# The experts' loop of a DeltaNet-Conformer-MoE layer: gate and up product of a block in one piece, down product last, and no row added for empty slots

## The chip, the core and the metric

The kernel runs on one core of a Trainium2 chip. The core has a matrix engine (TensorE, PE in the profile, with its weight loads shown as PEld), a vector engine (VectorE, DVE), a scalar engine (ScalarE, ACT), a general engine (GpSimd, POOL) and a queue for transfers (SyncE, SP). Each engine works through its own list of instructions in order and waits on semaphores for the others. The metric is the device time of one execution in microseconds (us). The kernel before takes 1718.21 us, the median of three runs from 1717.66 to 1718.78.

## What is computed

One layer on 1024 latent tokens of width 1024, with 256 context tokens: a mixer (gated DeltaNet heads beside a convolution branch), then a mixture of experts, then a final norm. The change lies in the mixture of experts. Each token picks 6 of 64 experts; an expert is a small gated network from 1024 to 256 and back. Cut to that:

```python
def expert_block(args):
    tok, e = args
    return swiglu(h_pad[tok], w_gate[e], w_up[e], w_down[e])   # (silu(h wg) * (h wu)) wd

out = lax.map(expert_block, (slot_tok.reshape(n_blocks, MOE_BLOCK), block_exp))
weighted = (out.reshape(n_slots, d) * slot_w[:, None]).astype(h.dtype)
routed = jnp.zeros((t + 1, d), h.dtype).at[slot_tok].add(weighted)[:t]
return (routed + swiglu(hf, s_gate, s_up, s_down)).reshape(bsz, n, d)
```

There are 1024 x 6 = 6144 pairs of a token and an expert. All data is float32.

## The kernel before

The first part of the kernel (the mixer, the router, the shared expert) is recorded into a planner, which puts the operations of each engine into an order by the durations and dependencies that are written beside them. The experts' loop, which the change is about, stands behind the planner's output and is written out by hand.

**Blocks.** The experts are ranked by how many tokens chose them, and the list `CAPS` gives each rank a fixed number of places. `plan` packs these places into 62 blocks of 128 slots. A block is either 128 slots of one expert, or is shared by two: 96 and 32 slots, or 64 and 64. `split_units` then cuts a shared block into units of 32 or of 64 slots; a unit becomes a matrix product that uses 32 or 64 columns of the array, at a column position of its own (`tile_position`). Of the 62 blocks, 35 are whole (128 columns), 17 run in units of 32 and 10 in units of 64. Mostly a shared block and a whole one take turns. The places add up to 7936 slots, and 6144 of them hold a row; the others are empty.

**The steps of one block**, with the tiles that name them in the profile:

- `b_onehot` (line 1807, DVE) and `b_slots` (`sl`, lines 1815 to 1818, PE and DVE) find which token stands in each slot.
- `b_index` (lines 1827 to 1846) works out, on DVE, the rows to gather (`ig`) and the rows to add to (`ic`), with a small product on PE for the second expert of a shared block, and has POOL issue the gather of the token rows into `xg` (four buffers).
- `b_xpose` (`xt`, lines 1856 to 1862) transposes the gathered rows on PE; DVE and ACT move them into `hg` (two buffers) with the modulation applied.
- `b_weights` (line 1868, DVE) picks the routing weight of each slot.
- `b_gate_up` (`gu`, line 1608, PE) multiplies by the gate and up weights, in eight steps over the input width that sum into one bank. It can be called for a part of the eight steps.
- `b_swish` (`sg`, lines 1612 and 1613, ACT and DVE) makes silu(gate) x up.
- `b_actT` (`at`, lines 1618 and 1619) transposes that on PE; ACT copies it into `aT`.
- `b_down` (`dn`, line 1628, PE) multiplies by the down weights; DVE scales the result into `ob` (line 1887, two buffers).
- `b_add` (line 1896, POOL) issues an indirect transfer that adds the rows of `ob` to an accumulator in device memory. There are two accumulators, `acc_d[0]` and `acc_d[1]`; while blocks are shared the adds take turns between them, and in the last blocks all go to `acc_d[0]`. An add waits for the landing of the one before it on the same accumulator.

A float32 product of 128 rows and 512 columns stands in the trace as two matrix instructions. So `gu` of a whole block is 16 instructions, `dn` is 8, and in units of 32 there are four times as many, which run side by side on different columns.

**Empty slots.** In an empty slot the arithmetic of `b_index` gives the row number 1024 + slot for both lists. The gather has a bounds check at 1023 and leaves such rows out. The add has none: the accumulators have 1152 rows, and empty slots add their (unused) row to the last 128. `constants` (lines 1601 to 1603) sets these 128 rows to zero beforehand, by a memset of `ob[0]` and two copies.

**Weights.** Six slots hold the weights of six experts (3 MB each). SP fetches the next expert when a slot is free; the loop appends a slot to `free` when the last block of its expert has been issued.

**The order in the loop.** Iteration `i` works on several blocks at once: swish, `at`, `dn` and add of block `i`, `gu` of block `i + 1`, `xt` of `i + 2`, `sl` and index of `i + 4`, one-hot of `i + 5`. Since every engine takes its instructions in the order in which they are written, the order of the calls in the loop is the order on PE:

```python
at(b_swish, i)
at(b_gate_up, i + 1, 0, 2)
at(b_actT, i)
at(b_gate_up, i + 1, 2, 4)
at(b_down, i)
at(b_add, i, 0, None)
...
at(b_slots, i + 4)
at(b_xpose, i + 2, 0)
at(b_xpose, i + 2, 1)
at(b_weights, i + 2)
at(b_gate_up, i + 1, 4, 6)
at(b_index, i + 4)
at(b_gate_up, i + 1, 6, 8)
at(b_onehot, i + 5)
```

The loop starts with `i = -1`, which runs only the parts for later blocks. Behind it the accumulators are read back and summed, and the final norm is computed and stored.

Of the kernel before, what the change touches and what calls it, by code (L numbers as in the profile page):

```python
# [8 lines left out]
F32 = mybir.dt.float32  # L9
# [4 lines left out]
OP = mybir.AluOpType  # L14
# [135 lines left out]
def hybrid_kernel(tc, a, out):  # L150
    nc = tc.nc
    V, S, G, PE, SY = nc.vector, nc.scalar, nc.gpsimd, nc.tensor, nc.sync
    top = ExitStack()

    w = {n: a[n][0] for n in a if n not in ('x', 'c', 'ctx', 'c_ctx', 'g_final')}
# [5 lines left out]
    dp = top.enter_context(tc.tile_pool(name="dram", bufs=1, space=DR))  # L161
# [357 lines left out]
    O = Order()  # L519
    N = SimpleNamespace()  # L520

    def adder(eng, lat):
        def add(dur, fn, r=(), w=(), low=0):
            O(eng, dur, fn, r, w, low, lat)
        return add

    DVE, ACT, POOL, TE, DMA = (adder(*u) for u in (("DVE", 0.2), ("ACT", 0.2), ("POOL", 0.2), ("PE", 0.2), ("DMA", 2.2)))
# [534 lines left out]
    O = Order()  # L1062
# [134 lines left out]

    st_r, st_o = ExitStack(), ExitStack()
    xn_d = dp.tile([1024, 1088], F32, name="xn_d")
    acc_d = [dp.tile([1152, 1024], F32, name=f"acc{i}") for i in range(2)]  # L1200
    rs2 = cp.tile([128, 8, 2], F32, name="rs2")
    osc = cp.tile([128, 8, 4], F32, name="osc")

# [388 lines left out]
    def constants():  # L1592
        G.iota(N.iof, pattern=[[1, 128]], base=0, channel_multiplier=0, allow_small_or_imprecise_dtypes=True)
        G.iota(N.ioc, pattern=[[0, 128]], base=0, channel_multiplier=1, allow_small_or_imprecise_dtypes=True)
        for t in range(8):
            G.memset(N.aux[:, t, 0:1], float(128 * t - 1024))
        G.memset(N.aux[:, :, 2:3], 1.0)
        G.tensor_copy(N.aux[:, :, 1:2], N.ioc[:, 0:1][:, None, :].to_broadcast([128, 8, 1]))
        G.tensor_scalar(N.s1024[:, 0:1], N.ioc[:, 0:1], 1024.0, None, op0=OP.add)
        G.tensor_scalar(N.s1024[:, 1:2], N.ioc[:, 0:1], -1.0, None, op0=OP.mult)  # L1600
        G.memset(N.ob[0], 0.0)
        for i in range(2):
            SY.dma_start(acc_d[i][1024:1152], N.ob[0])

    def gate_up(pgu, lhsT, units, wts, ks=range(8)):
        for k in ks:
# [116 lines left out]
    for k in range(5, 10):  # L1723
# [9 lines left out]
        w=["wsg1"])  # L1733
    DMA(3.0, lambda: SY.dma_start(slots[3][0][:, 1], uw.rearrange("(p k) f -> p k f", k=8)), r=["wsg1"],
        w=["wsg"])
    DMA(3.0, lambda: SY.dma_start(slots[3][1], dw.rearrange("(p k) f -> p k f", k=2)), r=["wsg1"], w=["wsd"])
    DMA(1.5, lambda: SY.dma_start(N.gt2b, gt_d[8:16].rearrange("k p -> (k p)").partition_broadcast(128)), r=["open2"],
        w=["gt2"])
    O("POOL", 3.0, constants, r=["open2"], w=["ap", "so00", "so01"], lat=3.0)
    for k in range(2):  # L1740
        POOL(2.5, lambda k=k: G.tensor_tensor(slots[3][1][:, k, :], slots[3][1][:, k, :], N.gt2b, op=OP.mult),
             r=["gt2"], w=["wsd"], low=1)
# [45 lines left out]
    def fetch_ready():  # L1788
        while nxt and free:
            fetch(nxt.pop(0))  # L1790
# [101 lines left out]
    def b_add(B, j0, j1):  # L1892

        for (o, n, r, ic) in B['dst'][j0:j1]:
            turn[0] = 1 - turn[0] if B['two'] else 0
            G.indirect_dma_start(out=acc_d[turn[0]], out_offset=bass.IndirectOffsetOnAxis(ap=ic[:n], axis=0),  # L1896
                                 in_=B['ob'][o:o + n], in_offset=None, compute_op=OP.add)

    def o_overflow():

# [52 lines left out]
    def at(f, i, *a_):  # L1953
        if 0 <= i < nblk:
            f(BL[i], *a_)
# [42 lines left out]
    for i in range(-1, nblk):  # L1998
        fetch_ready()
        if 0 <= i + 1 < nblk:  # L2000
            BL[i + 1]['wts'] = {r: slots[held[r]] for (_, _, r) in BL[i + 1]['u3']}
        at(b_swish, i)
        at(b_gate_up, i + 1, 0, 2)
        at(b_actT, i)
        at(b_gate_up, i + 1, 2, 4)
        at(b_down, i)
        at(b_add, i, 0, None)
        if i >= 0:
            for r in {r for (_, _, r) in BL[i]['u3']}:
                if last[r] == i:  # L2010
                    free.append(held.pop(r))
            fetch_ready()
        if i < 0:
            at(b_slots, 2)
            at(b_index, 2)
        at(b_slots, i + 4)
        at(b_xpose, i + 2, 0)
        at(b_xpose, i + 2, 1)
        at(b_weights, i + 2)
        at(b_gate_up, i + 1, 4, 6)  # L2020
        at(b_index, i + 4)
        at(b_gate_up, i + 1, 6, 8)
        at(b_onehot, i + 5)
    ms_.close()


# [8 lines left out]
    with tc.For_i(0, n_over) as it:  # L2035
        rr = V.value_load(N.rows[0:1, bass.ds(it, 1)], min_val=0, max_val=63)
        re = SY.value_load(N.rows[0:1, bass.ds(it + 128, 1)], min_val=0, max_val=63)
        load_expert(0, re)
        V.tensor_tensor(pcol, N.posr[:, :, bass.ds(rr, 1)],
                        N.basb[:, bass.ds(it, 1)][:, None, :].to_broadcast([128, 8, 1]), op=OP.subtract)  # L2040
        oh = N.oh[0]
        V.tensor_tensor(oh, N.iol[:, None, 0:128].to_broadcast([128, 8, 128]), pcol.to_broadcast([128, 8, 128]),
                        op=OP.is_equal)
        B = dict(i=0, two=False, oh=oh, segs=[(0, 128, 0)], u3=[(0, 128, 0)], wts={0: slots[0]})
        b_slots(B)
        b_index(B)
        V.tensor_copy(wsel, B['xg'][:, bass.ds(rr + 1024, 1)])
        B['wc'] = wsel
        b_xpose(B, 0)
        b_xpose(B, 1)  # L2050
        b_gate_up(B, 0, 8)
        b_swish(B)
        b_actT(B)
        b_down(B)
        b_add(B, 0, None)
# [54 lines left out]
```

## Time and profile before

| | |
|---|---|
| median of three runs | 1718.21 us (1717.66 to 1718.78) |
| the profiled execution | 1718.04 us |
| its span | 1716.1 us |
| mean granted clock of TensorE in it | 0.975 |
| experts' gate, up and down weights fetched | 64 transfers of 1024 KB each |
| gathers of token rows, adds of result rows | 62 and 89 indirect transfers |

The span is the time from the first to the last instruction of the profiled execution; the runs' times have some 2 us more around it. A row of the timeline is one or several instructions of the same kind in a row: start in us from the span's start, length, engine, line, operation, the tiles written and read, active rows and columns of the array for a weight load or product, shape, and a count. The length of a merged row of PE reaches to the modelled end of its last instruction, which is later than the start of the next row; so the time that a piece costs is best read from start to start. In brackets stands the idle time of the engine just before, and what ended it.

### The profile page before, as it was taken

To read this page: it belongs to the slowest core of one execution; us is meant where nothing else is said; L and a number is where in the kernel's file an instruction comes from. 1 tells how busy PE (TensorE), PEld (TensorE's weight loads), DVE (VectorE), ACT (ScalarE), POOL (GpSimd) and SP (SyncE) were. 2 spreads that over 40 slices of the span, in tenths; PEclk is the share of its full clock that TensorE was granted. 3 is DMA by queue.
4 is the path that set the end of the run, shared out by engine and by line. 5 is a ranking of instruction groups with operands and counts; after the bars stand their busy time and mean duration, and the time that the engine had idled before them with its cause. 6 is when DMAs were issued, how large, how long until landed. Compare 5 with 4: busy or idle time off the path is not lost. (4 is left out here: it accounts for less than half of the span.)

```text
span 1716.1 us, 23373 instructions
## 1 busy us (share of the span) xinstructions
PE 1599.0 (93%) x8380; PEld 931.8 (54%) x8380; DVE 974.5 (57%) x2156; ACT 498.4 (29%) x1096; POOL 526.2 (31%) x443
## 2 busy tenths in 40 slices
PE   5999999896898899799999999999999999999995
PEld 1556766574775899787544334344444344343442
DVE  2576997498884976887603444343434444343424
ACT  4541267832222123444212112111111111111212
POOL 2321232442242776631111323232222223232310
PEclk9999999898999999899999999999999999999998
DMA  9455112554445136666458999999999999999957
GB/s 321 156 184 173 44 59 72 160 154 145 144 132 187 50 111 209 217 208 218 164 202 305 326 335 336 319 364 307 332 374 364 327 333 318 327 385 347 355 126 259
DMA packets 150657, 405.39 MB, mean 236 GB/s; under 512 B 21359, under 2 KB 64780, under 8 KB 125580
## 3 DMA queue, kind: packets, MB, share of 16 engines
q1 hardware_dynamic: 130978, 340.39, 54.6%
q0 software_dynamic: 18288, 59.26, 14.5%
q10 hardware_dynamic: 1274, 4.23, 0.6%
q8 instruction: 67, 1.10, 0.3%
q14 instruction: 50, 0.41, 0.1%
HBM read 340.01 MB, written 71.95 MB: 240 GB/s over the span
## 5 line engine op out<-in xcount | busy, mean ns | idle before, releaser
L1608 PE MATMUL gu<-wg,hg 128*32 128x512 f32 (+2 forms) x1968 | 463.2, 599 | 1.6 <-ACT hg L1862 1.6
L1887 DVE SCALAR_TENSOR_TENSOR ob<-dn,wc,gt2b 128x512 f32<-128x512 f32 x124 | 93.1, 751 | 366.0 <-PE dn L1628 366.0
L1896 POOL DMA_INDIRECT acc<-ob,ic x89 | 134.5, 1512 | 527.5 <-DVE st L1818 466.9
L1608 PEld LDWEIGHTS gu<-wg,hg 128*32 128x32 f32 (+2 forms) x1968 | 148.7, 137 | 203.9 <-issue 159.0
L1628 PE MATMUL dn<-wd,sg 128*32 128x512 f32 (+2 forms) x984 | 226.8, 598 | 0.5 <-ACT sg L1619 0.5
L1862 ACT ACTIVATE hg<-xt,mf 128x128 f32<-128x128 f32 x248 | 93.2, 456 | 377.3 <-PE xt L1856 376.0
L1628 PEld LDWEIGHTS dn<-wd,sg 128*32 128x32 f32 (+2 forms) x984 | 78.0, 137 | 143.3 <-issue 142.6
L676 PE MATMUL bk<-hTh,whi 128*128 128x512 f32 (+1 forms) x320 | 125.0, 391 | 12.2 <-ACT ot L762 9.4
L676 PE MATMUL bk<-hTl,whi 128*128 128x512 f32 (+1 forms) x320 | 120.0, 375 | 0.0
L676 PE MATMUL bk<-hTh,wlo 128*128 128x512 f32 (+1 forms) x320 | 119.8, 374 | 0.0
L663 POOL TENSOR_TENSOR wlo<-wst,whi 128x512 fp32r<-128x512 f32 x40 | 66.6, 1673 | 162.5 <-ACT whi L662 147.1
L1860 DVE TENSOR_SCALAR hg<-xt,mf 128x128 f32<-128x128 f32 x248 | 84.4, 403 | 51.8 <-DMA acc<-hg 51.8
L419 DVE SCALAR_TENSOR_TENSOR ycv<-yg,cfw,ycv 128x64 f32<-128x64 f32 (+14 forms) x120 | 103.5, 863 | 5.7 <-ACT ycv L415 2.7
L1846 POOL DMA_INDIRECT xg<-xn_d,ig x62 | 76.6, 1236 | 64.9 <-issue 19.4
L676 PEld LDWEIGHTS bk<-hTh,whi 128*128 128x128 f32 x320 | 61.3, 192 | 32.4 <-ACT ot L762 9.8
L1807 DVE TENSOR_TENSOR oh<-posl 128x1024 bf16<-128x1024 f32 (+3 forms) x89 | 77.6, 897 | 0.0
L1856 PE MATMUL xt<-ident,xg 128*128 128x128 f32 x496 | 70.3, 285 | 0.0
L676 PEld LDWEIGHTS bk<-hTl,whi 128*128 128x128 f32 x320 | 61.5, 192 | 10.8 <-issue 1.0
L676 PEld LDWEIGHTS bk<-hTh,wlo 128*128 128x128 f32 x320 | 61.2, 191 | 11.2
L1612 ACT ACTIVATE sg<-gu 128x256 f32<-128x256 f32 x62 | 23.8, 383 | 135.1 <-PE gu L1608 135.1
L1613 DVE TENSOR_TENSOR sg<-sg,gu 128x256 f32<-128x256 f32 x62 | 26.1, 422 | 63.6 <-ACT sg L1612 63.6
L1856 PEld LDWEIGHTS xt<-ident,xg 128*128 128x128 f32 x496 | 60.3, 194 | 1.4 <-issue 1.4
(445 smaller groups left out, 2678.1 us busy)
## 6 DMA issues: line engine op xcount, KB each, us to landing
wg<-exp_w_gate SPq DMA_DIRECT2D x64, 1024.0 KB
wg<-exp_w_up SPq DMA_DIRECT2D x64, 1024.0 KB
wd<-exp_w_down SPq DMA_DIRECT2D x64, 1024.0 KB
wm<-w_mod SPq DMA_DIRECT2D x24, 1024.0 KB
wst<-w_in SPq DMA_DIRECT2D x48, 256.0 KB
kv<-kv_d SPq DMA_DIRECT2D x20, 512.0 KB
qf<-bounce SPq DMA_DIRECT2D x20, 256.0 KB
eb<-egr_d SPq DMA_DIRECT2D x18, 256.0 KB
```

The lines of the kernel that those rows point to most:

```text
L419: V.scalar_tensor_tensor(yc[:, lo:hi], yg[:, lo + d:hi + d], cfw[:, t * 4 + j:t * 4 + j + 1], yc[:, lo:hi], op0=OP.mult, op1=OP.add)
L663: POOL(1.6, lambda st=st, sl=sl: G.tensor_tensor(lo(sl), st, hi(sl).bitcast(F32), op=OP.subtract), r=[ks_, kh_], w=[kl_])
L676: PE.matmul(b[:, :n], l(k), r[:, k, t0:t0 + n], start=(k == 0 and i == 0), stop=(k == 7 and i == 2))
L1608: PE.matmul(pgu[o:o + n, :].rearrange("p (a f) -> p a f", a=2), lhsT(k, o, n), wts[r][0][:, :, k, :], start=(k == 0), stop=(k == 7), tile_ ...
L1628: PE.matmul(pd[o:o + n, :], aT[:, k, o:o + n], wts[r][1][:, k, hf * 512:(hf + 1) * 512], start=(k == 0), stop=(k == 1), tile_position=(0, ...
L1807: V.tensor_tensor(oh[:, :, o:o + n], N.iol[:, None, p0:p0 + n].to_broadcast([128, 8, n]), N.posr[:, :, r:r + 1].to_broadcast([128, 8, n]), ...
L1846: G.indirect_dma_start(out=xg, out_offset=None, in_=xn_d, in_offset=bass.IndirectOffsetOnAxis(ap=ig, axis=0), bounds_check=1023, oob_is_er ...
L1856: PE.transpose(pt[:, csl(q)], nth(B['xg'][:, 0:1024], 4 * j + q, 8), ident)
L1860: V.tensor_scalar(hg[:, k, :], pt[:, csl(q)], sc_[:, k:k + 1], sh_[:, k:k + 1], op0=OP.mult, op1=OP.add)
L1862: S.activation(hg[:, k, :], pt[:, csl(q)], AF.Identity, scale=sc_[:, k:k + 1], bias=sh_[:, k:k + 1])
L1887: V.scalar_tensor_tensor(ob[:, hs_], res[hf], B['wc'], N.gt2b[:, hs_], op0=OP.mult, op1=OP.mult)
L1896: G.indirect_dma_start(out=acc_d[turn[0]], out_offset=bass.IndirectOffsetOnAxis(ap=ic[:n], axis=0), in_=B['ob'][o:o + n], in_offset=None, ...
```

## The change

Four edits, all in `hybrid_kernel`:

- The loop's calls are put into another order. `at` of block `i` comes first, then slots, transposes, weights and one-hot of later blocks, then all eight steps of `gu` of block `i + 1` in one call, its swish, the index work, and last `dn` and add of block `i`.
- The add gets the bounds check that the gather has, so that rows from 1024 on are left out.
- The accumulators have 1024 rows instead of 1152.
- The memset of `ob[0]` and the two copies of zeros go, and with them the planner's note that `constants` writes `ob[0]` (`so00`, `so01`).

```diff
-    acc_d = [dp.tile([1152, 1024], F32, name=f"acc{i}") for i in range(2)]
+    acc_d = [dp.tile([1024, 1024], F32, name=f"acc{i}") for i in range(2)]
...
-        G.memset(N.ob[0], 0.0)
-        for i in range(2):
-            SY.dma_start(acc_d[i][1024:1152], N.ob[0])
...
-    O("POOL", 3.0, constants, r=["open2"], w=["ap", "so00", "so01"], lat=3.0)
+    O("POOL", 3.0, constants, r=["open2"], w=["ap"], lat=3.0)
...
-                                 in_=B['ob'][o:o + n], in_offset=None, compute_op=OP.add)
+                                 in_=B['ob'][o:o + n], in_offset=None, bounds_check=1023, oob_is_err=False,
+                                 compute_op=OP.add)
...
-        at(b_swish, i)
-        at(b_gate_up, i + 1, 0, 2)
         at(b_actT, i)
-        at(b_gate_up, i + 1, 2, 4)
+        if i < 0:
+            at(b_slots, 2)
+            at(b_index, 2)
+        at(b_slots, i + 4)
+        at(b_xpose, i + 2, 0)
+        at(b_xpose, i + 2, 1)
+        at(b_weights, i + 2)
+        at(b_onehot, i + 5)
+        at(b_gate_up, i + 1, 0, 8)
+        at(b_swish, i + 1)
+        at(b_index, i + 4)
         at(b_down, i)
         at(b_add, i, 0, None)
...
-        if i < 0:
-            at(b_slots, 2)
-            at(b_index, 2)
-        at(b_slots, i + 4)
-        at(b_xpose, i + 2, 0)
-        at(b_xpose, i + 2, 1)
-        at(b_weights, i + 2)
-        at(b_gate_up, i + 1, 4, 6)
-        at(b_index, i + 4)
-        at(b_gate_up, i + 1, 6, 8)
-        at(b_onehot, i + 5)
```

## The prediction, made before the changed kernel ran

> **What bounds the kernel now.** I read the page first (busy shares, slices, clock), then one window over the experts' loop, then the waits of TensorE in it, then its timeline piece by piece.
>
> ```profile
> span 1716.1 us, 23373 instructions
> PE 1599.0 (93%) x8380; PEld 931.8 (54%) x8380; DVE 974.5 (57%) x2156; ACT 498.4 (29%) x1096; POOL 526.2 (31%) x443
> ...
> PEclk9999999898999999899999999999999999999998
> DMA  9455112554445136666458999999999999999957
> ...
> q0 software_dynamic: 18288, 59.26, 14.5%
> ```
> ```profile
> 921.77:1680.22 758.45, 756.99 (x4055) 316.32 (x4054) 317.45 (x958) 137.66 (x364) 204.91 (x146) 1.00 0.95 324
> ```
> ```profile
> PE at L1618 <- DVE sg L1613: 0.9, 1, 0.9
> PE dn L1628 <- ACT sg L1619: 0.5, 1, 0.5
> ```
> The window runs from the end of block 0's `gu` to the end of the last `dn`. Its columns are length, then busy time of PE, PEld, DVE, ACT, POOL, then granted clock, DMA share, GB/s. PE is busy 756.99 of 758.45 us at clock 1.00, and the list of its waits in that time has two entries, both in the last block. So PE's own order of work sets 758 of 1718 us. The DMA share is as high (0.95), but a full DMA queue only counts when somebody waits for it, and PE never waits for a transfer here. A busy PE is not a PE without loss, so I looked at when its pieces start.
>
> The last blocks need no smaller tile (`128*128` throughout); columns are start, length, engine, line:
>
> ```profile
> 1656.38 3.60 PE L1628 MATMUL dn<-wd,sg 128*128 128x512 f32 x8
> 1659.81 1.05 PE L1856 MATMUL xt<-ident,xg 128*128 128x128 f32 x8
> 1660.70 5.32 PE L1608 MATMUL gu<-wg,hg 128*128 128x512 f32 x12
> 1665.85 0.39 PE L1618 MATMUL at<-ident,sg 128*128 128x128 f32 x2
> 1666.08 1.88 PE L1608 MATMUL gu<-wg,hg 128*128 128x512 f32 x4
> ```
> From start to start: `dn` 3.43 us for 8 instructions, `gu` 5.15 for 12 (0.429 each in both), `xt` 0.89, `at` 0.23. No change of kind costs anything. Now two blocks in which a 32-column block alternates with a whole one:
>
> ```profile
> 929.45 0.34 PE L1815 MATMUL sl<-auxb,oh 128*128 128x3 bf16 x8
> 929.65 1.14 PE L1856 MATMUL xt<-ident,xg 128*128 128x128 f32 x8
> 930.72 5.55 PE L1608 MATMUL gu<-wg,hg 128*32 128x512 f32 x36
> 936.12 0.39 PE L1618 MATMUL at<-ident,sg 128*128 128x128 f32 x2
> 936.34 1.88 PE L1608 MATMUL gu<-wg,hg 128*128 128x512 f32 x4
> 938.15 3.64 PE L1628 MATMUL dn<-wd,sg 128*32 128x512 f32 x32
> 941.73 0.36 PE L1815 MATMUL sl<-auxb,oh 128*128 128x3 bf16 x8
> 941.94 1.14 PE L1856 MATMUL xt<-ident,xg 128*128 128x128 f32 x8
> 942.92 1.88 PE L1608 MATMUL gu<-wg,hg 128*128 128x512 f32 x4
> 944.73 0.23 PE L1827 MATMUL sl<-st,ident 128*32 128x3 f32 x2
> 944.88 3.84 PE L1608 MATMUL gu<-wg,hg 128*128 128x512 f32 x20
> 948.65 0.51 PE L1618 MATMUL at<-ident,sg 128*128 128x128 f32 x2
> 949.09 1.92 PE L1608 MATMUL gu<-wg,hg 128*32 128x512 f32 x16
> 950.94 3.70 PE L1628 MATMUL dn<-wd,sg 128*128 128x512 f32 x8
> 954.48 0.34 PE L1815 MATMUL sl<-auxb,oh 128*128 128x3 bf16 x8
> 954.68 0.58 PE L1856 MATMUL xt<-ident,xg 128*128 128x128 f32 x3
> ```
> Four 32-column instructions run side by side, so 32 of them take as long as 8 whole ones. The same work is longer wherever **the column width changes**. `xt` takes 0.98 before whole `gu` (941.94) and 1.07 before narrow `gu` (929.65). Whole `gu` x4 takes 1.72 before whole `dn` (all-whole rows) and 1.81 before narrow `dn` (936.34). `at` takes 0.22 between whole pieces and 0.44 between narrow ones (948.65). Narrow `dn` takes 3.58, whole `dn` after narrow `gu` 3.54, against 3.43. From these differences: the piece before a change is 0.094 longer; the piece after it 0.104 (whole product), 0.046 (narrow product), 0.11 (`at`), 0.01 (`sl`) or nothing (the index product at 944.73). So one change costs 0.20 into a whole product, 0.14 into a narrow one, 0.21 into `at`, 0.105 into `sl`, 0.094 into the index product.
>
> As a check I laid the 62 blocks of `plan` out in the program's order and priced base times and changes so: 718.0 of work, 38.4 of changes, and 1.9 for the two waits at the end (each with its handovers) make 758.3, against 758.45 measured.
>
> **The change part by part.** (1) *The order on PE.* An iteration was part of the next block's `gu`, `at`, `gu`, `dn`, `sl`, `xt`, `gu`, index, `gu`; it becomes `at`, `sl`, `xt`, whole `gu`, index, `dn`. The three 128-wide pieces now stand together, and one block's `gu` no longer runs into the next block's. Laying out both orders by the code, changes of width fall from 248 to 113. By place:
> - around `at`, 27 narrow blocks: 27 x (0.207 + 0.14) = 9.4 gone
> - one block's `gu` into the next's: 24 x 0.197 + 25 x 0.14 = 8.2 gone
> - out of the index product back into `gu`: 20 x 0.197 + 0.14 = 4.1 gone
> - into `dn`: 24 x 0.197 + 25 x 0.14 = 8.2 becomes 25 x 0.197 + 12 x 0.14 + 0.2 = 6.8, since the index product now stands where a change was due: 1.4 gone
> - out of `dn`: 27 times into `at` (0.207) where it was into `sl` (0.105): 2.8 added
> - `xt` into narrow `gu` and into the index product: unchanged
>
> Sum: 20.3, and 20.4 without rounding. The instructions stay the same in number. Bounds: with only the 0.094 ahead of a change saved, 135 x 0.094 = 12.7; with the dearest price, 135 x 0.207 = 27.9. I take 20.4, because the prices add up to the measured loop.
>
> The Trainium skill ("TensorEngine Tiling (Array Packing)", Tiling Modes) says that changing the tiling mode, but not the tile, drains TensorE; it gives no price. At one price for each drain, 38.4 over the loop's changes, the sum would be about 21; the rows above show unequal prices, so 20.4 stands.
>
> (2) *New and lost waits on PE.* Start and end of the loop:
>
> ```profile
> 912.09 1.37 DVE L1860 TENSOR_SCALAR hg<-xt,mf 128x128 f32<-128x128 f32 x4 [51.81 <-DMA acc<-hg]
> 912.61 3.67 PE L1608 MATMUL gu<-wg,hg 128*128 128x512 f32 x8 [1.60 <-ACT hg L1862]
> ...
> 921.87 0.38 ACT L1612 ACTIVATE sg<-gu 128x256 f32<-128x256 f32 x1 [2.28 <-PE gu L1608]
> 922.29 0.42 DVE L1613 TENSOR_TENSOR sg<-sg,gu 128x256 f32<-128x256 f32 x1 [0.62 <-ACT sg L1612]
> ```
> ```profile
> 1675.75 0.51 PE L1618 MATMUL at<-ident,sg 128*128 128x128 f32 x2 [0.93 <-DVE sg L1613]
> 1676.79 3.70 PE L1628 MATMUL dn<-wd,sg 128*128 128x512 f32 x8 [0.53 <-ACT sg L1619]
> ```
> ```profile
> 1681.56 1.56 POOL L1896 DMA_INDIRECT acc<-ob,ic  x1 [7.54 <-DVEq L2035]
> ```
> Once running, `at` needs the swish of its block, which takes about 1.1 (0.84 on ACT and DVE, and handovers); `dn` of the block before covers it with 3.43. In block 0 there is no such `dn`: `at` waits, and `sl`, `xt` and the second block's `gu` are queued behind it. Its `gu` also ends no earlier than now (921.8): DVE holds `hg` until 912.09, and `sl`, `xt` then go ahead of `gu`. That is 1.1 added. In the last block `dn` of block 60 now covers the swish: the first wait (0.93, 1.1 with handover) goes, and the second, for `aT`, stays.
>
> In the tail the last two adds come closer. Both go into one accumulator, and the code makes the second wait for the first's landing; behind it stand the final loads. `dn` 61 now ends at E = 1680.2 (the window's end) and add 61 is issued at E+1.35. After the change `dn` 60 ends 4.5 ahead of E (`at` with its wait 1.04, `dn` 3.43), so add 60 is issued at E-3.2. It lands in 6.0 (minimum below) less 0 to 1.4 for empty slots (1792 of 7936); at 0.7, add 61 goes at E+2.2 and is itself 0.7 shorter. Net +0.2, between -1.2 and +1.5.
>
> (3) *Gather and fetch, at nothing.*
>
> ```profile
> 932.86 1.32 POOL L1846 DMA_INDIRECT xg<-xn_d,ig  x1 [0.55 <-ACT hg L1862]
> ```
> ```profile
> DMA to landing us min/median/max: 5.6/11.3/13.7
> ```
> ```profile
> DMA to landing us min/median/max: 6.0/9.8/11.6
> ```
> ```profile
> SPq L1774 <- PE gu L1608: 325.8, 29, 26.1
> ```
> The first landing row is the gathers', the second the adds'. A gather is issued 3.2 us after its iteration's `xt` (932.86 against 929.65) and used by the `xt` two blocks on, so it had 21.8. Its index arithmetic now stands on DVE behind the swish, that is, behind the whole `gu`: issue at 0.23 + 0.21 + 1.0 + 6.9 + 1.1 and about 1.0 for arithmetic and dispatch, 10.5 into an iteration of 11.9, which leaves 2 x 11.9 - 10.5 + 0.65 = 14.0. That covers the worst landing by 0.3 and the median by 2.7. On POOL the gather now goes ahead of its iteration's add rather than right behind it, and the add before is 9 us old, so I expect landings below 11. The weights' queue waits for freed slots, not the other way; a down weight is fetched some 3 us later, and the six weight slots let the fetch run several experts ahead. DVE and ACT have 58% and 82% of the loop idle, so the earlier one-hot and the moved evictions hide under `gu`.
>
> (4) *Empty slots.* 59.26 MB on q0 is 7936 slots x 4096 B of adds and 6144 rows x 4352 B of gathers; 1792 added rows (7.3 MB) vanish. Nobody on the path waits for an add before the tail, so I count nothing beyond (2). The zeroing that goes (one memset, two copies) lies in the stage ahead of the loop, off any wait I found: 0, between -1 and +1, since an edge of the planner goes with it.
>
> Sum: -20.4 + 1.1 - 1.1 + 0.2 = -20.2. Against the profiled execution's 1718.04 (span 1716.1 and 1.9 around it; the median of the runs is 1718.21) that is **1697.8 us**.
>
> **Rivals.**
> - *The gather becomes the bound (slower).* If it lands later than 14.0, each iteration waits half the excess, since two iterations lie between. Some 58 of them eat the gain from a landing of 14.7 on. At 16.0 the loop is 58 us longer: 1756. For it: margin 0.3 over the worst row, DMA share 0.95. Against: the shorter queue ahead, fewer bytes. 5%.
> - *Only part of a change's cost goes*, because the array also drains at a new piece of the same width: 12.7 saved, 1705.5. Against: whole `at` at 1665.85 costs nothing extra. 5%.
> - *The clock falls.* `at`, `sl` and `xt` now stand together, 1.4 us. If transposes counted as idle, the clock could halve, and 58 pieces of some 3 us at half clock cost 1.5 each: +87 and -20, 1785. Against: ahead of the `gu` at 912.61 PE stood still for 1.60 (its row above), and the clock stayed at 9 tenths or more in that slice. 2%.
>
> The Trainium skill ("TensorE: Matmul & The Clock Gate", Part 4) has that rule, transposes not counting as busy, beside a window of about 3.4 us in Part 1; by that the cluster is too short to matter, and the trace agrees.
>
> - *The skip does nothing*: adds take as long as now. Only the tail loses: +1.4, 1699. 5%.
>
> **How the numbers follow.** The forecast's case (1694 to 1702) has 83%; the partial case and small gather waits reach to 1706. The range is 1693 to 1706. What a measurement here can tell from no change is about 0.2%, 3.4 us. Faster 0.93 (forecast, partial, skip, and a little of the gather case), same 0.03, slower 0.04 (rest of the gather case, clock).
>
> **What would show it.** In the new timeline: narrow `gu` as one piece of 6.9 to 7.1 us, `at` straight followed by `sl` and `xt`, blocks of about 11.9; one PE wait near 922 (about 1), the 0.93 at the end gone; q0 at 51.9 MB; gather landings under 14.0 and no PE wait on `xg`. Wrong would be: waits of `xt` on a gather, a clock under 1.00 in the loop, or `at` behind narrow `dn` costing more than 0.21.

## The result and the profile after

The changed kernel takes 1698.78 us, the median of four runs from 1697.16 to 1700.06, against 1718.49 for the kernel before on the same chip: a ratio of 0.9885, interval 0.9868 to 0.9902. Its profiled execution took 1699.74 us, with a span of 1698.0 us at a mean clock of 0.973.

The page of the changed kernel, with the lines that answer to those shown of before:

```profile
span 1698.0 us, 23460 instructions
PE 1576.9 (93%) x8380; PEld 945.3 (56%) x8380; DVE 973.1 (57%) x2156; ACT 498.4 (29%) x1096; POOL 530.9 (31%) x442
...
PEclk9999999997999999899999999999999999999997
DMA  9455122455434336665358899998999999999947
...
q0 software_dynamic: 18288, 51.94, 12.3%
```

PE runs the same 8380 instructions and is busy 22.1 us less; the span is 18.1 us shorter. Queue q0, which carries the gathers and the adds, moved 51.94 MB instead of 59.26. The next two fences are the window from the end of block 0's `gu` to the end of the last `dn` (columns: length, busy PE, PEld, DVE, ACT, POOL, granted clock, DMA share, GB/s), and the waits of PE from the first `xt` on (what waits, for what, us in total, times, longest).

```profile
920.31:1658.99 738.68, 737.20 (x4057) 330.39 (x4056) 319.91 (x964) 137.71 (x364) 211.40 (x147) 1.00 0.92 322
```
```profile
PE sl L1812 <- DVE st L1814: 2.5, 1, 2.5
PE at L1615 <- DVE ig L1834: 0.8, 1, 0.8
PE dn L1625 <- ACT sg L1616: 0.5, 1, 0.5
PE xt L1853 <- DMA xg<-xn_d,ig: 0.2, 1, 0.2
```

The same stretch took 758.45 us before and takes 738.68 now, and PE is busy for all but 1.5 us of it, at clock 1.00. So the loop is still bound by PE's own order, and the gain is less busy time rather than fewer waits: only four waits are left, three of them at the start (the longest ahead of this window) and one at the end. (Lines are 3 or 4 lower than before.) The timeline of PE over two blocks shows where the time went:

```profile
933.89 0.39 PE L1615 MATMUL at<-ident,sg 128*128 128x128 f32 x2
934.12 0.34 PE L1812 MATMUL sl<-auxb,oh 128*128 128x3 bf16 x8
...
942.35 3.60 PE L1625 MATMUL dn<-wd,sg 128*32 128x512 f32 x29
945.88 0.50 PE L1615 MATMUL at<-ident,sg 128*128 128x128 f32 x2
946.22 0.34 PE L1812 MATMUL sl<-auxb,oh 128*128 128x3 bf16 x8
...
947.49 7.07 PE L1605 MATMUL gu<-wg,hg 128*32 128x512 f32 x64
954.50 3.70 PE L1625 MATMUL dn<-wd,sg 128*128 128x512 f32 x8
958.03 0.39 PE L1615 MATMUL at<-ident,sg 128*128 128x128 f32 x2
```

From `at` to `at` two blocks take 958.03 - 933.89 = 24.14 us; in the rows of before, the same two steps from `sl` to `sl` took 954.48 - 929.45 = 25.03. The narrow `gu` is one piece of 7.01. `at` still pays for the narrow `dn` ahead of it (945.88 to 946.22 is 0.34, against 0.23 at 933.89), but nothing behind it does.

At the end of the loop, POOL's and SP's rows:

```profile
1655.86 1.56 POOL L1893 DMA_INDIRECT acc<-ob,ic  x1 [8.97 <-DVE ob L1884]
1662.71 1.56 POOL L1893 DMA_INDIRECT acc<-ob,ic  x1 [5.28 <-DMA acc<-ob,ic]
```
```profile
1669.59 4.03 SPq L2067 DMA_DIRECT2D wg<-acc  x8
```

The last add now waits 5.28 us for the landing of the add before it, and is issued 3.6 us behind the last `dn`; the final loads come 6.88 us after it. Before, the last add was issued at 1681.56 and the loads came at 1688.44, also 6.88 later.

### The profile page after: what moved, and what is told of

The parts are those of the page before. It is cut to its first block, busy times and chain, and to the rows that moved or that the text cites. A ratio compares the mean times of both kernels' runs of the same rounds, so it can differ in the third digit from the quotient of the medians.

```text
span 1698.0 us, 23460 instructions
## 1 busy us (share of the span) xinstructions
PE 1576.9 (93%) x8380; PEld 945.3 (56%) x8380; DVE 973.1 (57%) x2156; ACT 498.4 (29%) x1096; POOL 530.9 (31%) x442
## 3 DMA queue, kind: packets, MB, share of 16 engines
q1 hardware_dynamic: 130690, 339.34, 54.6%
q0 software_dynamic: 18288, 51.94, 12.3%
## 5 line engine op out<-in xcount | busy, mean ns | idle before, releaser
L1605 PE MATMUL gu<-wg,hg 128*32 128x512 f32 (+2 forms) x1968 | 437.3, 594 | 0.0
L1605 PEld LDWEIGHTS gu<-wg,hg 128*32 128x32 f32 (+2 forms) x1968 | 159.4, 137 | 231.6 <-issue 228.3
L1893 POOL DMA_INDIRECT acc<-ob,ic x89 | 151.4, 1701 | 152.2 <-DVE st L1815 105.5
L1843 POOL DMA_INDIRECT xg<-xn_d,ig x62 | 65.3, 1054 | 417.4 <-issue 123.5
L1625 PEld LDWEIGHTS dn<-wd,sg 128*32 128x32 f32 (+2 forms) x984 | 82.2, 137 | 121.0 <-issue 111.4
L1616 ACT ACTIVATE sg<-at 128x256 f32<-128x256 f32 x62 | 23.8, 384 | 220.3 <-PE at L1615 216.3
```

The lines of the kernel that those rows point to most:

```text
L1605: PE.matmul(pgu[o:o + n, :].rearrange("p (a f) -> p a f", a=2), lhsT(k, o, n), wts[r][0][:, :, k, :], start=(k == 0), stop=(k == 7), tile_ ...
L1625: PE.matmul(pd[o:o + n, :], aT[:, k, o:o + n], wts[r][1][:, k, hf * 512:(hf + 1) * 512], start=(k == 0), stop=(k == 1), tile_position=(0, ...
L1843: G.indirect_dma_start(out=xg, out_offset=None, in_=xn_d, in_offset=bass.IndirectOffsetOnAxis(ap=ig, axis=0), bounds_check=1023, oob_is_er ...
```

## The experiments

To compare the runs I cut each profiled execution into the same parts. X is the start of the first `xt` ahead of the loop; E is the start of the last `dn` instruction plus 0.43 us; then come the issue of the last add, the start of the final loads, and the end of the span. The medians are of all runs of a kernel, the parts are of its one profiled execution, which can lie a few us beside the median (1712.42 for "`at` between"). Each ratio is to runs of the kernel before on the same chip.

| kernel | median us | ratio, interval | X | X to E, the loop | E to last add | to final loads | to the end |
|---|---|---|---|---|---|---|---|
| before | 1718.49 | | 909.96 | 770.37 | 1.23 | 6.88 | 27.66 |
| changed | 1698.78 | 0.9885 [0.9868, 0.9902] | 908.43 | 750.66 | 3.62 | 6.88 | 28.43 |
| order alone | 1701.41 | 0.9903 [0.9888, 0.9918] | 908.39 | 750.46 | 3.73 | 7.13 | 28.04 |
| skip alone | 1718.31 | 0.9991 [0.9981, 1.0] | 910.34 | 770.01 | 1.23 | 6.84 | 28.41 |
| one width, old order | 1689.65 | 0.9825 [0.981, 0.984] | 914.23 | 738.51 | 1.23 | 7.49 | 27.44 |
| one width, new order | 1688.82 | 0.9819 [0.9804, 0.9834] | 910.19 | 740.62 | 3.42 | 6.73 | 27.12 |
| changed, again | 1699.38 | 0.9887 [0.9872, 0.9902] | 906.87 | 751.77 | 3.96 | 6.84 | 28.19 |
| `at` between | 1707.71 | 0.9926 [0.9911, 0.9942] | 912.74 | 758.25 | 4.76 | 7.00 | 27.95 |
| late gather | 1807.57 | 1.051 [1.0491, 1.0529] | 908.43 | 860.41 | 3.72 | 6.84 | 28.50 |
| delayed `dn` | 1703.51 | 0.9902 [0.9888, 0.9915] | 910.55 | 746.48 | 9.01 | 6.87 | 27.66 |
| delayed `dn`, mended | 1695.71 | 0.9876 [0.9858, 0.9894] | 909.59 | 746.23 | 3.78 | 6.99 | 27.68 |
| changed, third time | 1700.38 | 0.9896 [0.9879, 0.9912] | 911.17 | 751.44 | 3.60 | 6.77 | 28.29 |

X lies behind a stage of some 900 us that most of these kernels share, and it wanders between 906.9 and 914.2, also in three executions of one kernel (908.43, 906.87, 911.17). A difference of two or three us in the total says little by itself; the loop's length and the tail say more.

**The order alone.** Against the kernel before: the new order of calls, but the accumulators of 1152 rows, the zeroing and the add without a bounds check, as before.

```diff
-        at(b_swish, i)
-        at(b_gate_up, i + 1, 0, 2)
         at(b_actT, i)
-        at(b_gate_up, i + 1, 2, 4)
...
+        at(b_gate_up, i + 1, 0, 8)
+        at(b_swish, i + 1)
+        at(b_index, i + 4)
+        at(b_down, i)
+        at(b_add, i, 0, None)
```

> The new order alone: accumulators of 1152 rows, the zeroing and the unchecked add are back. Theory (width changes on PE are the whole gain): from xt of block 0 to the end of the last dn 750.6 us as in the changed kernel (770.3 before), time 1698 to 1700, not distinguishable from the changed kernel; the last add lands 5.7 to 6.0 after its issue as there. Rival (the skipped rows pay for part of it through less traffic): 1702 or more, and the loop longer than 751.5.

Measured: 1701.41 us, a loop of 750.46, 0.2 from that of the changed kernel, and the tail of the changed kernel too (last add at E + 3.73, loads 7.13 later). The time is 1.4 above the expected 1698 to 1700, so the loop decides between the theory and its rival (longer than 751.5): the order carries the whole gain in the loop, and also the loss in the tail.

**The skip alone.** Against the kernel before: the bounds check, the smaller accumulators and no zeroing, in the old order.

```diff
-    acc_d = [dp.tile([1152, 1024], F32, name=f"acc{i}") for i in range(2)]
+    acc_d = [dp.tile([1024, 1024], F32, name=f"acc{i}") for i in range(2)]
...
-                                 in_=B['ob'][o:o + n], in_offset=None, compute_op=OP.add)
+                                 in_=B['ob'][o:o + n], in_offset=None, bounds_check=1023, oob_is_err=False,
+                                 compute_op=OP.add)
```

> The bounds check, the smaller accumulators and the missing zeroing alone, in the old order of the loop. Theory: loop 770.3 as before, time 1717 to 1718.5; a start of the loop that is up to 1.5 us earlier if the zeroing stood in the way ahead of it (xt of block 0 at 908.4 in the changed kernel, 909.96 before). Rival (less traffic pays): 1715 or less.

Measured: 1718.31 us, ratio 0.9991 with an interval from 0.9981 to 1.0; loop 770.01 against 770.37. The loop starts at 910.34, no earlier than before, so the zeroing did not stand in its way. The bytes do go (its page's line first), and the gathers' landing (second fence, its median 11.3 before) gets shorter; nobody on the path waited for either.

```profile
q0 software_dynamic: 18288, 51.94, 12.8%
```
```profile
DMA to landing us min/median/max: 5.6/9.9/12.8
```

**One width, in both orders.** The cause that the prediction named is the change of column width. If it is the cause, then without narrow pieces the two orders must take the same time. These two kernels leave out the product of the second expert of every shared block: each block is one product of 128 columns with its first expert's weights. Everything else, the index work, gathers, adds and weight fetches, stays. The same edit was made to the kernel before (old order) and to the changed kernel (new order):

```diff
-    BL = [dict(..., u3=[(o, n, r) for (o, n, r, p0) in split_units(u)])
+    BL = [dict(..., u3=[(0, 128, u[0][2])])
...
-            for r in {r for (_, _, r) in BL[i]['u3']}:
+            for r in {r for (_, _, r) in BL[i]['segs']}:
```

> Old order, with every block multiplied as one whole 128-column product by the weights of its first expert: the second expert's gate, up and down products of a shared block are left out. Its weights are still fetched. Theory: width changes fall from 248 to 52, all of them around the index product; loop 31.3 shorter than before, time 1687 (1685 to 1689). Rival (pieces cost something at their ends whatever their width): the loss of 38 stays and the time is 1710 or more.

> New order, with the same products left out as in whole_before. Theory: also 52 width changes, so the order brings nothing: 10.7 shorter than the changed kernel, 1688 (1686 to 1690), within 2 us of whole_before. Rival (the order itself, fewer and longer pieces, or the skipped rows are what pays): 15 to 20 us faster than whole_before, 1668 to 1672.

Measured: loops of 738.51 in the old order and 740.62 in the new, 1689.65 and 1688.82 us in all. The order that was worth 19.7 us in the loop is worth nothing (it is 2.1 longer: its start has 1.2 us more of waits, and one stretch of 3.41 us, 913.52 to 916.93, at half clock). The old order with one width, PE's timeline:

```profile
945.61 1.45 PE L1608 MATMUL gu<-wg,hg 128*128 128x512 f32 x3
946.99 0.23 PE L1827 MATMUL sl<-st,ident 128*32 128x3 f32 x2
947.14 3.70 PE L1608 MATMUL gu<-wg,hg 128*128 128x512 f32 x8
950.68 0.39 PE L1618 MATMUL at<-ident,sg 128*128 128x128 f32 x2
950.90 1.88 PE L1608 MATMUL gu<-wg,hg 128*128 128x512 f32 x4
952.62 3.60 PE L1628 MATMUL dn<-wd,sg 128*128 128x512 f32 x8
```

Here `gu` is cut by `at` just as before, and from start to start `at` costs 0.22 and the four steps behind it 1.72, the price of uncut work. Only the index product, the last narrow piece left, still costs: `gu` x8 behind it takes 3.54 where eight take 3.43. Both loops came within 0.7 us of the lengths worked out from the prices (739.1 and 740.0). That the pieces are fewer, or that the three transposing steps stand together, is not what pays.

**`at` between.** Against the changed kernel, one pair of changes back: `at` again inside `gu`, between its second and third step.

```diff
-        at(b_actT, i)
...
-        at(b_gate_up, i + 1, 0, 8)
+        at(b_gate_up, i + 1, 0, 2)
+        at(b_actT, i)
+        at(b_gate_up, i + 1, 2, 8)
```

> The changed kernel with at alone put back between the second and third step of gu, for all blocks. Theory (price by width change): 27 narrow gu are cut, 167 changes of width in place of 113, loop 6.6 longer by the prices and 1.1 shorter because the swish of block 0 is covered again: 756.1, time 1703 to 1706; at takes 0.22 between whole pieces and 0.43 between narrow ones. Rival (every cut of a product costs): at costs 0.4 in all 62 blocks, loop 760 or more.

> The changed kernel once more, beside the others of this call: 1697 to 1700, loop (xt of block 0 to the end of the last dn) 750.6.

Measured: 1707.71 us, a loop of 758.25, against 751.77 for the changed kernel run beside it: 6.5 us given back. Both loops hold some 1.5 us at a fallen clock at their start (the last section shows it), which nearly cancels in the difference. The forecast of 756.1 and 1703 to 1706 was too low: the 6.6 by the prices is there, but the 1.1 that the start was to save is not, since another `sl` waits 1.2 there, and the lower clock was not in the sum. The pieces, from its timeline:

```profile
952.78 1.92 PE L1605 MATMUL gu<-wg,hg 128*32 128x512 f32 x16
954.64 0.50 PE L1615 MATMUL at<-ident,sg 128*128 128x128 f32 x2
955.07 5.36 PE L1605 MATMUL gu<-wg,hg 128*32 128x512 f32 x48
...
965.07 1.88 PE L1605 MATMUL gu<-wg,hg 128*128 128x512 f32 x4
966.79 0.39 PE L1615 MATMUL at<-ident,sg 128*128 128x128 f32 x2
967.02 5.32 PE L1605 MATMUL gu<-wg,hg 128*128 128x512 f32 x12
```

Between narrow pieces `at` takes 0.43 from start to start, between whole ones 0.23: the same instruction pays by its neighbours. The tail is longer as well (last add at E + 4.76).

**A late gather.** The rival by which the kernel could have become slower: the gathers as the bound. Against the changed kernel, the index work and the gather stand behind `dn` and the add.

```diff
-        at(b_index, i + 4)
         at(b_down, i)
         at(b_add, i, 0, None)
+        at(b_index, i + 4)
```

> The changed kernel with the index work (and so the gather) of block i + 4 put behind dn and add of block i. The gather is then issued some 16 us into its iteration and has 8 to 9 us until its xt, where it had 14. Theory (the gather's cover is used up, and each iteration waits half of what the landing exceeds the time left): landings of 10 to 11 as before the change, since the gather is right behind the adds again, PE waits of xt for the gather of 0.5 to 1.5 us a block, time 1730 to 1790. Rival (the cover was never thin, landings shrink to 6): under 1705 and no such waits.

Measured: 1807.57 us, where 1730 to 1790 had been expected; the loop is 109.8 us longer. The direction was right and the size was too small. PE's waits, POOL's issue rows and PE's rows for one pair of blocks:

```profile
PE xt L1853 <- DMA xg<-xn_d,ig: 55.5, 27, 4.2
PE sl L1812 <- DVE sl L1831: 19.7, 25, 0.9
```
```profile
1303.05 1.88 POOL L1843 DMA_INDIRECT xg<-xn_d,ig  x1 [0.30 <-issue]
1313.54 1.58 POOL L1893 DMA_INDIRECT acc<-ob,ic  x1 [8.61 <-DVE st L1835]
1315.43 1.06 POOL L1843 DMA_INDIRECT xg<-xn_d,ig  x1 [0.30 <-issue]
```
```profile
1313.76 0.34 PE L1812 MATMUL sl<-auxb,oh 128*128 128x3 bf16 x8 [0.64 <-DVE sl L1831]
1315.23 1.13 PE L1853 MATMUL xt<-ident,xg 128*128 128x128 f32 x8 [1.13 <-DMA xg<-xn_d,ig]
```
```profile
DMA to landing us min/median/max: 5.7/9.6/12.1
```

The gather follows its add on POOL. The one issued at 1303.05 is for the `xt` at 1315.23, which stood still for the last 1.13 us, so some 11.0 were free; landings go up to 12.1 (that row covers the 19 of 62 gathers whose landing this trace holds). In the changed kernel the landings are shorter, although the gather is issued later in its iteration than before:

```profile
DMA to landing us min/median/max: 3.9/8.6/10.6
```

The order alone has the same median, 8.6, with all 59.26 MB on q0; so the place ahead of the add is enough to bring it down from 11.3 (in the old order the empty slots alone took it to 9.9). The size has two parts. The waits in the list above make 75.2, and only 55.5 of them are for gathers: the edit also puts the index product straight ahead of the next block's `sl`. Both use the one bank `sl`, so `sl` waits until DVE (L1831) has copied the index product out, 25 times. The rest is busy time, from the window over this loop:

```profile
920.00:1768.00 848.00, 771.43 (x4059) 341.41 (x4059) 322.11 (x964) 137.68 (x364) 204.47 (x147) 0.97 0.81 281
```

PE is busy 771.4 us here at a mean granted clock of 0.97, where the changed kernel needed 737.2 at 1.00: 34.2 more, and 75.2 + 34.2 = 109.4. The expectation had priced the waits for gathers alone; the last section comes back to the clock.

**A delayed `dn`.** A step beyond the changed kernel: `dn` of block `i - 1` instead of `i`, slots and index one block earlier, `at` behind `xt`. In a row of blocks that take turns, the narrow `gu` of block `i + 1` then stands beside the narrow `dn` of block `i - 1`. By the count it leaves 92 changes of width instead of 113.

```diff
-        at(b_slots, i + 4)
+        at(b_slots, i + 5)
...
+        at(b_actT, i)
...
-        at(b_index, i + 4)
-        at(b_down, i)
-        at(b_add, i, 0, None)
+        at(b_index, i + 5)
+        at(b_down, i - 1)
+        at(b_add, i - 1, 0, None)
```

> The changed kernel with dn and add of block i - 1 in iteration i (so that the dn behind a gu mostly has its width), slots and index one block earlier (i + 5, for the same reason), and at behind xt (so that sl and xt cover the swish of the first block). Theory (price by width change): 92 changes in place of 113 and cheaper ones, 6.2 less by the prices, 1.1 less at the start and 0.8 at the end: loop 742.5, time 1689 to 1692. Rival (weight slots are held one block longer, and the weights come too late): waits of gu or dn for exp_w transfers, 1697 or more.

Measured: the loop is 746.48, 5.3 shorter than that of the changed kernel beside it, but the whole takes 1703.51. The time lies where the rival had put it (1697 or more), but its sign is missing: none of PE's four waits, 5.2 us in all and all at the start, is for a weight. The loop is 4.0 longer than the 742.5 expected, most likely by these waits and by one stretch of 3.41 us at half clock behind them (916.05 to 919.46), not by the prices. They show here from the other side: the narrow `gu` ahead of another narrow piece takes 6.89 (948.91 to 955.80), against the 7.01 ahead of a whole `dn`. What the loop gained, the tail took back; POOL's last rows:

```profile
1651.16 1.56 POOL L1893 DMA_INDIRECT acc<-ob,ic  x1 [8.96 <-DVE ob L1884]
1658.73 1.56 POOL L1893 DMA_INDIRECT acc<-ob,ic  x1 [6.01 <-issue]
1666.03 1.56 POOL L1893 DMA_INDIRECT acc<-ob,ic  x1 [5.73 <-DMA acc<-ob,ic]
```

At the end two `dn` follow each other without a `gu` between, three adds to one accumulator stand in line, and each waits for the landing of the one before, 7.3 to 7.6 us from issue to issue. The last goes at E + 9.0.

**The delayed `dn`, mended.** Against the delayed `dn`: each `dn` back in its own iteration from block 54 on, and slots of block 4 behind block 0's `gu`.

```diff
+    turn_at = nblk - 8
...
+        done = [i - 1] if i < turn_at else [i]
+        if i == turn_at:
+            at(b_down, i - 1)
+            at(b_add, i - 1, 0, None)
+            done = [i - 1, i]
         at(b_gate_up, i + 1, 0, 8)
...
+        at(b_down, done[-1])
+        at(b_add, done[-1], 0, None)
```

> The delayed down product with its two faults mended: from block 54 on each down product stands in its own block again (the product of block 53 goes ahead of the gate/up piece of block 55, both whole), so that the last adds are a block apart as in the changed kernel, and slots of block 4 stand behind the first gate/up product, where they cover the swish of block 0. Theory (PE's order with 92 changes of width instead of 113, and no start wait): 6.1 us less for changes and about 1.1 less for the start, so a loop of about 743.4 us from the first transposes to the end of the last down product, the tail as in the changed kernel (add 61 3.6 us behind the last down product), and 7 us less in all: 1690 to 1694, with no wait of PE on a gather or a weight. Rival (a delayed down product holds weight slots and accumulator rows longer, and that costs what the order saves): the loop no shorter than 749, and 1697 or more.

> The changed kernel again, as a measure on this chip beside the mended delay: 1697 to 1701 us, loop 750 to 752.

Measured: 1695.71 us, where 1690 to 1694 had been expected, against 1700.38 for the changed kernel beside it. The tail is mended (last add at E + 3.78). The loop is 746.23, 5.2 shorter than the changed kernel's, where 743.4 had been expected. Its start holds the missing time:

```profile
913.27 0.35 PE L1812 MATMUL sl<-auxb,oh 128*128 128x3 bf16 x8 [2.45 <-DVE st L1814]
913.49 1.95 PE L1853 MATMUL xt<-ident,xg 128*128 128x128 f32 x8
915.37 0.27 PE L1824 MATMUL sl<-st,ident 128*32 128x3 f32 x2
915.56 7.70 PE L1605 MATMUL gu<-wg,hg 128*128 128x512 f32 x16
...
933.70 0.34 PE L1812 MATMUL sl<-auxb,oh 128*128 128x3 bf16 x8 [1.41 <-DVE sl L1831]
```

One slot chain still waits 1.41 for DVE, and behind the wait of 2.45 the transposes take 1.88 instead of 0.97 and `gu` 7.55 instead of 6.97, that is 1.5 at a lower clock. 743.4 + 1.4 + 1.5 = 746.3. It is the fastest of the kernels that leave nothing out, by 4.7 us in the medians; the two intervals of the ratio to before overlap (0.9858 to 0.9894 and 0.9879 to 0.9912), so the small lead over the changed kernel rests on the loops of one execution each, 746.2 against 750.7 to 751.8.

## Why the prediction was right, and which term was off

The prediction said 1697.8 and the profiled execution took 1699.74, the median 1698.78. By its steps:

- *What bounds the kernel.* It holds before and after: PE is busy 737.20 of 738.68 us. The account of the loop as work plus changes of width plus waits, made on before alone, gave 738.0 for the stretch that measured 738.68.
- *(1) The order, -20.4.* The stretch got 758.45 - 738.68 = 19.8 shorter. The experiments confirm the cause and not only the sum: with one width the order is worth nothing, and with `at` put back 6.5 us come back. The prices by neighbour held, too: `at` behind narrow `dn` 0.34, as 0.23 plus 0.11. The rival by which only part of the price goes (12.7) is out.
- By the one price for every switch that the prediction worked out beside the Trainium skill ("TensorEngine Tiling (Array Packing)", Tiling Modes), the sum was about 21. The measured 19.8 doesn't decide between that and 20.4, but the rows do: the pieces pay unequal prices.
- *(2) Waits at the start.* `at` waited 0.78 where it had been foreseen (1.1 had been put down for it), and the `sl` of block 3, at 912.17, took over the wait that `gu` had had: from X to the swish of block 0 it is 11.9 us before and 12.0 now (909.96 to 921.87, 908.43 to 920.42).
- *(2) The tail, +0.2: this is the term that was mis-sized.* From E to the final loads it was 1.23 + 6.88 before and is 3.62 + 6.88 now, +2.4. Add 60 is issued 3.2 us ahead of E, as predicted. But the step that counted 6.0 "less 0 to 1.4 for empty slots" for its landing, and add 61 as "itself 0.7 shorter", failed: here an add with skipped rows takes as long as a full one. The rows' packets show it: in each of the last four adds the last row ends 5.7 to 5.8 us after issue with 91 or 92 rows, and 5.7 to 5.9 with 128 before. From issue to issue the last two adds are 6.85 apart where 5.3 had been counted, 6.1 to the landing and 0.7 of handover; with the 0.7 that add 61 did not save, that is the missing 2.2. And the loads stand at 6.88 behind the last add in both. The rival "the skip does nothing", at +1.4 for the tail, was nearer, and it too counted too little, for the handover between the landing and the next issue.
- *(3) Gather and fetch, at nothing.* Right. Of 62 gathers the slowest landed in 10.6 us where about 14 were free; one `xt` waited 0.17, at the start. The late gather shows what lay behind the margin: with some 11 us left instead of 14, PE waits 55.5 us for gathers.
- *(4) Empty slots, at nothing on the path.* Right: alone they change the time by 0.1%, with an interval that touches none.
- *The clock.* No loss in the running loop: 1.00 in the window above. The sentence on the Trainium skill's rule ("TensorE: Matmul & The Clock Gate", Part 4) stands for the 1.4 us of transposing work in each block; beside waits it is another matter: in the two later executions of this kernel one stretch of 3.41 us at the loop's start ran at half clock, which no term of the sum had (last section).

The sum of the parts: X 1.5 earlier, loop 19.7 shorter, tail 2.4 longer, the end 0.8 longer: 18.0, and the spans differ by 18.1. So of the two us between forecast and profiled execution, the tail explains 2.2 and the loop 0.7; the earlier X and the later end, -0.8 together, are within what these two show between executions. That they made the total agree a little better is luck.

## What to carry to other kernels

When an engine is busy all the time, lay its pieces out from start to start and sort each kind by its neighbours: what a piece costs beside another kind of piece is a price that an order of the program can save, and the busy share hides it, since the price counts as busy time too. Count the changes in each order before building one; here a count from the code and prices from one trace gave the loop within 0.7 us. And look at the end of a loop by itself, since what spreads out work (adds a block apart) in the middle may be lost in the last iterations, where it can eat a whole gain, as the delayed `dn` did.

## What the runs showed of the hardware that was not expected

- **Skipped rows of an indirect add saved bytes, and at the end of the loop no time.** 59.26 MB became 51.94, but the last row of the last adds ends in the same 5.7 to 5.9 us, with 91 or with 128 rows. In the running loop the adds' median landing does fall, from 9.8 to 8.9 us in the old order and from 10.4 to 9.9 in the new one, and nobody waits for it there. What skipping more than 37 of 128 rows would do was not tried.
- **Waits at the start of the loop can cost PE half its clock for 3.41 us behind them.** There `sl` waits 2.5 us for DVE. In the first execution of the changed kernel the transposes behind it took 0.97; in the second, after the same wait, this:

```profile
910.60 0.35 PE L1812 MATMUL sl<-auxb,oh 128*128 128x3 bf16 x8 [2.50 <-DVE st L1814]
910.81 1.95 PE L1853 MATMUL xt<-ident,xg 128*128 128x128 f32 x8
912.55 7.70 PE L1605 MATMUL gu<-wg,hg 128*128 128x512 f32 x16
```
```profile
910.70:913.50 2.80, 2.80 (x18) 2.28 (x18) 2.25 (x12) 0.70 (x3) 1.04 (x1) 0.50 1.01 402
```

The granted clock is 0.50 in that window, and `xt` and `gu` together take 1.5 us longer. The record of the granted clock in the twelve traces shows what differs. Every low stretch in the loops lasts 3.41 us or twice that, and within one execution all of them start on one grid of steps of 3.41 us, which lies elsewhere in each execution. In the second execution the step ahead of the low one runs from 907.08 to 910.49 and holds nearly the whole wait: PE is busy for 1.02 us of it. In the first the grid cuts the wait at 911.16; PE is busy for 1.92 and 2.40 us of the two steps that share it, and the clock stays at 1.00. A long wait is not needed either. In the third execution `at`, `sl` and `xt` have waits of 0.77 and 0.43 between them:

```profile
924.17 1.79 PE L1853 MATMUL xt<-ident,xg 128*128 128x128 f32 x8 [0.43 <-issue]
925.89 1.08 PE L1605 MATMUL gu<-wg,hg 128*32 128x512 f32 x4
```

Here `xt` takes 1.72, against 1.09 at the same place in the first execution, and the clock is 0.50 from 924.50 on. In the step before (921.09 to 924.50) PE was busy for 2.21 us, more than a third of it with transposes. Counted over the loops of all twelve traces, PE spent at most 42% of the step ahead of a low one on anything but transposes (23 steps); where it spent more, the next step was always at 1.00, and where it spent less, it was sometimes one and sometimes the other. So a wait in PE's order, and transposes beside it, should be priced at up to 1.5 us more than the wait's length. In the late gather, with its 52 waits, thirteen such stretches make 54.6 us at half clock, and PE is busy for most of it: some 25 of the 34 us of added busy time. An estimate for the other 9: a piece ahead of a wait is busy to its own end, where otherwise the next piece starts sooner (`sl` 0.34 instead of 0.20), some 0.15 for each of 52 waits, which is 8; and the count gives 121 changes of width instead of 113, 1.8 more by the prices.
- **The gathers landed sooner (8.6 against 11.3 us in the median) when they were issued ahead of the adds on POOL**, with the same bytes (the order alone), though the DMA share of the loop stayed above 0.9. The adds behind them landed later, 10.4 against 9.8.
